# Two attention units share a PSUM bank for their values, and the mLSTM's small sums are done once for two units

## The chip, the cores and the metric

The kernel runs on one core of one Trainium2 chip. The metric is the device time of one execution in microseconds (us). Before the change it was 3861.58 us, the median of three runs (3859.82 to 3863.74).

## The reference, cut to what matters

The reference is a long chain of layers on 512 latent tokens and 256 context tokens of 1024 channels. Two places of it are touched. In the first layer, two attentions of 8 heads each run over the same 768 tokens; latent rows see all 768 keys, context rows the 256 context keys alone:

```python
def attend(q, k, v):
    ...
    s = jnp.einsum('bqgrd,bsgd->bgrqs', qi, k).astype(jnp.float32) * scale
    p = jax.nn.softmax(s, axis=-1).astype(v.dtype)
    return jnp.einsum('bgrqs,bsgd->bqgrd', p, v)
```

"GQA" has 8 query heads on 2 key/value heads of 64 channels; "MLA" has 8 heads with keys of 96 channels and values of 64. In the second layer an mLSTM runs in both directions over the sequence, and its result is divided by a sum of its own weights:

```python
den = w_inter * jnp.einsum('bhd,bhtd->bht', n, qc) + jnp.sum(s, axis=-1)
h = num / jnp.maximum(jnp.abs(den), jnp.exp(-m_t))[..., None]
```

## The kernel before, in words

One function builds each layer, and every engine executes its instructions in the order in which the Python code issues them. There is no scheduler: `pipeline` (L1660) walks over steps, and in each step calls a list of stages, each with a lag, so that stage `f` with lag 3 handles unit `u - 3` in step `u`. The order of that list is the order on every engine.

**Attention** (`run`, L1918, called for GQA at L2022 and for MLA at L2117). A unit is one head and one block of 128 query rows: 8 heads x 6 blocks = 48 units per attention. Blocks 0 to 3 are latent ("heavy", 768 keys), 4 and 5 context ("light", 256 keys). Per unit:

- `S`: scores into a two-bank PSUM tile `D` on TensorE, one step ahead (L1894 and L1895 for GQA; L1914 to L1916 for MLA).
- `X`: maximum and bias on VectorE (L1942, L1943), exponential on ScalarE (L1946).
- `R`: reciprocal of the sum on VectorE (L1950), scaling on GpSimd (L1951).
- `Tr`: transposes of the probabilities on TensorE (L1962) into banks `A` (4) and `B` (2).
- `CpB`, `CpA`: copies of these into the tile `pT`, by ScalarE (L1967) and VectorE (L1972).
- `PV`: the product with the values (L1981), six matmuls for a heavy unit and two for a light one, accumulating in bank `V`. Its stationary operand has 128 columns: two heads' values side by side (MLA), or the one head's values twice (GQA, copied twice by `twice`, L1794). So all 128 rows of the result are computed, and only the 64 of the unit's own head are used.
- `Ev`: the 64 rows are split into a rounded high part (L1988) and the rest (L1989), both on VectorE.
- `prep`, `preH`, `preL`: transposes of the next head's queries and keys, and their split.

There is one bank `V`: the next `PV` cannot begin before `Ev` has read the last one.

**mLSTM** (`ml_heads`, L2327). A unit is one head and one block of 128 rows, 8 x 4 = 32 units. `decay` makes exponentials on ScalarE two steps ahead (L2402 to L2405), `S_` the scores on TensorE (L2392, L2393), and `M` (L2407) multiplies them on VectorE in three instructions with running sums (L2414). Then follow four small instructions on one or two columns: L2415 adds two sums, L2418 takes the magnitude, L2419 the maximum with `em`, L2420 the reciprocal. With these, `R` scales and adds on GpSimd (L2425 to L2428), `Tr` transposes (L2436), `CpA` copies on ScalarE (L2440), `PV` multiplies with the values (L2447), `Ev` reads the result on ScalarE (L2454, L2455). GpSimd makes the masks of the next head too (L2364). After the last unit, `wout_k` gives TensorE matmuls of the output projection between the last stages.

Of the kernel before, what the change touches and what calls it, by code (L numbers as in the profile page):

```python
# [12 lines left out]
F32 = mybir.dt.float32  # L13
F32R = mybir.dt.float32r
AF = mybir.ActivationFunctionType
# [166 lines left out]
class Kernel:  # L182
# [1503 lines left out]
    def attn(self):  # L1686
# [103 lines left out]
        def to(dst, d0):  # L1790

            return lambda t, n: dst[:, t, d0:d0 + n]

        def twice(t, n):  # L1794

            return G2[:, t, 128:].rearrange("p (g u n) -> p u g n", g=2, u=2)
# [11 lines left out]
        for g, cut in enumerate(cuts):  # L1808
            n = sum(c[2] for c in cut)
            o = self.six()  # L1810
            self.nat(("ai", g), 4, x, range(6), [b[:, :n] for b in o], mid=mid[g > 0], extra=extra[g],
                     ada=(0, 1, 1, 1)[g])
            for t in range(6):
                for dst, c0, m in cut:
                    a, b = dst(t, m), o[t][:, c0:c0 + m]
                    if dst is twice:
                        b = b.rearrange("p (g n) -> p g n", g=2).unsqueeze(1).to_broadcast([P, 2, 2, 64])
# [31 lines left out]

        def prep_g(h, i, b):  # L1850

            if (i == 1 and 2 <= h < 4) or (i == 2 and h == 3):
# [12 lines left out]
            for c in range(2):  # L1865
                o = slice(t0 * P, t1 * P)
                r.append((b[c * 64:c * 64 + 64, :(t1 - t0) * P],
                          (qs[c * 64:c * 64 + 64, c, o], qs[64 - c * 64:128 - c * 64, c, o])))
            return r

        def lat_kv(h, i, b):

            g = [self.v("mla_kva_g", c) for c in range(2)]
            if i == 1:
                c = h - 2
# [42 lines left out]
        def run(prep, scores, value, sc, out, bg, tail):  # L1918


            self.psum(A=2, B=1, V=1)
            esW, pW = self.pool(self.nm("attW"), "left")
            units = [(h, t) for h in range(8) for t in range(6)]
            U = [dict(W=768 if t < 4 else 256) for h, t in units]

            def S(u):
                h, t = units[u]
                d = U[u]
                d["s"] = b = self.bank("D").rearrange("p a b -> p (a b)")
                if t == 4 and h < 7:  # L1930
                    U[u - 1]["pre"] = prep(h + 1, 2, b[:, 0:512])
# [31 lines left out]

            def CpB(u):
                d = U[u]
                d["p"] = p = pW.tile([P, TT], F32, tag="pT", bufs=3, name=self.nm("pT"))
                nc.scalar.activation(p[:, T:], d.pop("B")[:, :TC], AF.Copy)  # L1967

            def CpA(u):
# [2 lines left out]
                    nc.vector.tensor_copy(d["p"][:, :T], d.pop("A"))  # L1972

            def PV(u):
                h, t = units[u]
                d = U[u]
                d["o"] = q = self.bank("V")[:, 0:P]
                p = d.pop("p")
                j0 = 6 - d["W"] // P
                for j in range(j0, 6):  # L1980
                    nc.tensor.matmul(q, value(h, j), p[:, j * P:(j + 1) * P], start=j == j0, stop=j == 5)  # L1981

            def Ev(u):
                h, t = units[u]
                r = slice(h % 2 * 64, h % 2 * 64 + 64)
                q = U[u].pop("o")[r]
                hi, lo = (z[r, h // 2, t * P:(t + 1) * P] for z in out)
                nc.vector.tensor_copy(hi, q)  # L1988
                nc.vector.tensor_tensor(lo, q, hi, ALU.subtract)  # L1989

            def preT(u):
                h, t = units[u]
                if t < 2 and h < 7:
                    U[u]["pre"] = prep(h + 1, t, self.bank("A"))
# [9 lines left out]
                    else:  # L2004
                        nc.vector.tensor_tensor(dst[1], src, dst[0], ALU.subtract)

            for i in range(3):
                U[0]["pre"] = prep(0, i, self.bank("AAV"[i]))
# [318 lines left out]
    def ml_heads(self, x, esi, pi, es7, openx):  # L2327
# [67 lines left out]
        def decay(u):  # L2395
            h, j = units[u]
            d, E, dm = U[u], st[h]["U"], st[h]["dm"]
            e = til([P, 1152], "mE", 5)
# [8 lines left out]
        def M(u):  # L2407
            h, j = units[u]
            d = U[u]
            q, f, b = d.pop("s"), d["f"], d["b"]  # L2410
            den = til([P, 4], "mden", 3)
            n = d["Wb"] - TC
            for i, (o, c) in enumerate(((b[:, n:], slice(0, TC)), (b[:, :n], slice(d["c"], TT)), (f, slice(0, d["Wf"])))):
                nc.vector.scalar_tensor_tensor(o, q[:, c], 0.125, o, ALU.mult, ALU.mult, accum_out=den[:, 2 - i:3 - i])  # L2414
# [70 lines left out]
        def last(f):  # L2485
            return at(3, f)
# [4 lines left out]
        for c in range(8):  # L2491
# [4 lines left out]
            if c == 7:  # L2496
# [12 lines left out]
        decay(0)  # L2509
        decay(1)  # L2510
        S_(0)
        self.pipeline(len(units), ((3, CpA), (4, Ev), (-2, decay), (0, at(0, keysH, 1)), (0, at(1, queriesH, 1)),
                                   (10, last(n6h)), (5, last(n2)), (0, M), (0, at(1, keysL, 1)),
                                   (0, at(2, queriesL, 1)), (8, last(n3)), (12, last(n6l)), (1, R),
                                   (0, at(1, masks, 1)), (9, last(n4)), (-1, S_), (2, Tr), (3, PV), (9, last(n5)),
                                   (0, at(2, load, 2)), (3, at(3, load_v, 2)), (4, last(load_o))),
                      lambda i: self.wout_k("mw", hl, min(i, 6)) if i < 6 or i == 8 else None)
        es.close()
        esp.close()
        self.psum(M=2, A=2)  # L2520
# [233 lines left out]
```

## Time and profile before

| | |
|---|---|
| median of three runs | 3861.58 us |
| the profiled execution's own time | 3859.96 us |
| its span, first to last instruction | 3858.2 us |
| TensorE / VectorE / ScalarE / GpSimd busy, whole span | 95% / 68% / 41% / 19% |
| granted TensorE clock, whole span | 0.981 |
| GQA, first to last maximum (L1942) | 178.45 to 291.96 us |
| MLA, first to last maximum (L1942) | 354.98 to 476.63 us |
| mLSTM, first to last reciprocal (L2420) | 1367.66 to 1486.69 us |

The busy time of TensorE is a sum over stages of very different make, and a matmul's duration in the trace includes its latency, so that neighbours overlap. What a matmul costs is the distance between the starts of two neighbours. A matmul of two plain float32 operands stands twice in the trace, as two passes, each with its own weight load ("PEld"): 6 matmuls of one heavy `PV` are 12 records. Transposes are one pass.

### The profile page before, as it was taken

The numbers are of one execution on the slowest core, as the hardware profiler recorded it, in microseconds if no ns is written. First come the engines' busy times: TensorE is split into PE (matmuls) and PEld (weight loads), VectorE is DVE, ScalarE is ACT, GpSimd is POOL, SyncE is SP. The second block draws the span as 40 slices with busy tenths as digits, with TensorE's granted clock in tenths as the row PEclk, the third lists the DMA queues.
The fourth block names the chain that finished last, engine by engine and source line by source line (L and its number), as shares of the span: only waits on it lengthen the run. The fifth ranks groups of instructions, "written<-read, shape, count | busy, mean of one in ns | idle before, by whom it ended". The sixth has DMA issues, their size and how long they took to land. (4 is left out here: it accounts for less than half of the span.)

```text
span 3858.2 us, 54617 instructions
## 1 busy us (share of the span) xinstructions
PE 3656.6 (95%) x21148; PEld 3150.7 (82%) x21148; DVE 2621.0 (68%) x4287; ACT 1577.4 (41%) x2606; POOL 720.7 (19%) x755
## 2 busy tenths in 40 slices
PE   7898999999999978999999998999999999889999
PEld 5887978888887777877789886788977998678898
DVE  7887877765646286544477777677765777766776
ACT  2354523222225275422344447444443444464443
POOL 6334231000012074100100016100020000460000
PEclk8999999999999999999999999999999999899999
DMA  5300043433422442233333322333334333213332
GB/s 176 107 1 23 1 148 95 125 112 118 137 68 88 139 134 77 82 90 90 90 98 102 96 78 81 97 87 96 95 114 124 98 99 99 83 42 102 98 103 75
DMA packets 570400, 363.48 MB, mean 94 GB/s; under 512 B 17719, under 2 KB 546605, under 8 KB 570141
## 3 DMA queue, kind: packets, MB, share of 16 engines
q1 hardware_dynamic: 564317, 346.21, 30.7%
q0 software_dynamic: 3520, 9.59, 0.8%
q8 instruction: 167, 2.74, 0.3%
q10 hardware_dynamic: 2304, 4.20, 0.3%
q14 instruction: 92, 0.75, 0.1%
HBM read 345.72 MB, written 14.20 MB: 93 GB/s over the span
## 5 line engine op out<-in xcount | busy, mean ns | idle before, releaser
L135 DVE TENSOR_TENSOR wl<-ws,wh 128x1024 fp32r<-128x1024 f32 (+3 forms) x474 | 583.3, 1240 | 313.6 <-ACT wh L132 311.2
L132 ACT ACTIVATE wh<-ws 128x1024 fp32r<-128x1024 f32 (+3 forms) x474 | 457.6, 978 | 588.5 <-DVE ws L454 257.3
L562 PE MATMUL D<-ah,wl 128*128 128x256 f32 x1344 | 380.2, 283 | 11.1 <-DVE wl L135 11.1
L560 PE MATMUL D<-ah,wh 128*128 128x256 f32 x1344 | 377.1, 281 | 1.6 <-DVE gu L602 1.6
L561 PE MATMUL D<-al,wh 128*128 128x256 f32 x1344 | 376.4, 280 | 0.9 <-DVE al L495 0.9
L539 PE MATMUL M<-hz,wh 128*128 128x512 f32 x704 | 279.9, 398 | 2.2 <-DVE xT L545 2.2
L540 PE MATMUL M<-hz,wh 128*128 128x512 f32 x704 | 280.4, 398 | 1.0 <-DVE hz L638 0.9
L541 PE MATMUL M<-hz,wl 128*128 128x512 f32 x704 | 278.8, 396 | 0.0
L562 PEld LDWEIGHTS D<-ah,wl 128*128 128x128 f32 x1344 | 252.8, 188 | 18.5 <-DVE wl L135 18.5
L341 POOL TENSOR_TENSOR acc<-acc,t 128x512 f32<-128x512 f32 x36 | 46.9, 1303 | 1171.4 <-ACT t L340 1171.4
L560 PEld LDWEIGHTS D<-ah,wh 128*128 128x128 f32 x1344 | 252.9, 188 | 6.0 <-ACT wh L132 1.9
L561 PEld LDWEIGHTS D<-al,wh 128*128 128x128 f32 x1344 | 252.8, 188 | 5.0 <-DVE al L495 1.3
L321 PE MATMUL D<-ah,wl 128*128 128x512 f32 (+1 forms) x616 | 242.8, 394 | 7.0 <-DVE wl L135 7.0
L317 PE MATMUL D<-ah,wh 128*128 128x512 f32 (+1 forms) x616 | 244.7, 397 | 3.0 <-ACT wh L132 2.7
L319 PE MATMUL D<-al,wh 128*128 128x512 f32 (+1 forms) x616 | 242.8, 394 | 0.8 <-POOL al L2676 0.6
L303 POOL TENSOR_TENSOR hl<-t,hh 128x768 fp32r<-128x768 f32 (+1 forms) x44 | 70.0, 1590 | 797.9 <-ACT hh L302 737.1
L1349 DVE SCALAR_TENSOR_TENSOR as<-ws,S,as 128x256 f32<-128x256 f32 x448 | 202.7, 504 | 3.5
L560 PE MATMUL E<-ah,wh 128*128 128x256 f32 x672 | 188.9, 281 | 6.8 <-ACT t L590 4.0
L562 PE MATMUL E<-ah,wl 128*128 128x256 f32 x672 | 189.9, 283 | 4.7 <-DVE wl L135 4.7
L561 PE MATMUL E<-al,wh 128*128 128x256 f32 x672 | 188.1, 280 | 0.0
L317 PE MATMUL D<-x7h,wh 128*128 128x512 f32 (+1 forms) x464 | 183.8, 399 | 3.0 <-ACT x7h L2671 1.6
L321 PE MATMUL D<-x7h,wl 128*128 128x512 f32 (+1 forms) x464 | 181.4, 394 | 1.1 <-DVE wl L135 1.1
(711 smaller groups left out, 9696.6 us busy)
## 6 DMA issues: line engine op xcount, KB each, us to landing
ws<-in_ffn_w_up_dram SPq DMA_DIRECT2D x104, 512.0 KB
ws<-in_ada_w_dram SPq DMA_DIRECT2D x88, 512.0 KB
t<-in_ffn_w_down_dram SPq DMA_DIRECT2D x128, 256.0 KB
ws<-in_ffn_w_gate_dram SPq DMA_DIRECT2D x88, 256.0 KB
ws<-in_ffn_w_up_dram SPq DMA_DIRECT2D x88, 256.0 KB
wz<-in_ffn_w_gate_dram SPq DMA_DIRECT2D x56, 256.0 KB
wz<-in_ffn_w_up_dram SPq DMA_DIRECT2D x56, 256.0 KB
ws<-in_ffn_w_down_dram SPq DMA_DIRECT2D x32, 384.0 KB
```

What stands on the lines that cost most here:

```text
L132: self.nc.scalar.activation(h[:, :n], t[:, :n], AF.Copy)
L135: self.nc.vector.tensor_tensor(l[:, :n], t[:, :n], h[:, :n], ALU.subtract)
L317: nc.tensor.matmul(o, wh[:, kw + k], xh[:, k0 + k, s], start=a, stop=False)
L319: nc.tensor.matmul(o, wh[:, kw + k], xl[:, k0 + k, s], start=False, stop=False)
L321: nc.tensor.matmul(o, wl[:, kw + k], xh[:, k0 + k, s], start=False, stop=z)
L539: nc.tensor.matmul(q, wh[:, k], h[:, 0, i], start=a, stop=False)
L540: nc.tensor.matmul(q, wh[:, k], h[:, 1, i], start=False, stop=False)
L541: nc.tensor.matmul(q, wl[:, k], h[:, 0, i], start=False, stop=z)
L560: nc.tensor.matmul(o, wh[:, u, k], xh(k0 + k, s), start=start and k == 0, stop=False, skip_group_check=True)
L561: nc.tensor.matmul(o, wh[:, u, k], xl(k0 + k, s), start=False, stop=False, skip_group_check=True)
L562: nc.tensor.matmul(o, wl[:, u, k], xh(k0 + k, s), start=False, stop=stop and k == 3, skip_group_check=True)
L1349: nc.vector.scalar_tensor_tensor(t, w[:, kk], c, t, ALU.mult, ALU.add)
```

## The change

`PV` waits for two units and works on both at once. The stationary operand is now the unit's own 64 columns of values; the first unit's result goes to partitions 0 to 63 of bank `V`, the second's to 64 to 127, and the matmuls of the two alternate. In the built program these matmuls carry a tile of 128 x 64 at column 0 or 64 of the array, where all others around them carry 128 x 128. GQA's units are reordered so that a pair is two heads with the same block (`by_head`); an MLA pair is two blocks of one head. `Ev` becomes `EvH` on ScalarE (lag 5) and `EvL` on VectorE (lag 6), for GQA one instruction of 128 rows for the pair, for MLA two of 64. The tile `pT` has four buffers instead of three. In the mLSTM the four small instructions are issued in every second step, for two units, and everything from `R` on comes one step later; `mE` has six buffers instead of five.

```diff
-        G2 = pG.tile([P, 6, 384], F32, name="rawG2")
+        G2 = pG.tile([P, 6, 256], F32, name="rawG2")
...
-        cuts = (((to(G, 0), 0, 384),), ((to(G, 384), 0, 128), (to(G2, 0), 128, 128), (twice, 256, 128)),
+        cuts = (((to(G, 0), 0, 384),), ((to(G, 384), 0, 128), (to(G2, 0), 128, 128), (to(G2, 128), 256, 128)),
...
-            units = [(h, t) for h in range(8) for t in range(6)]
+            units = ([(h + c, t) for h in (0, 2, 4, 6) for t in range(6) for c in range(2)] if by_head else
+                     [(h, t) for h in range(8) for t in range(6)])
...
             def PV(u):
+                if u % 2 == 0:
+                    return
                 h, t = units[u]
-                d = U[u]
-                d["o"] = q = self.bank("V")[:, 0:P]
-                p = d.pop("p")
-                j0 = 6 - d["W"] // P
+                U[u]["o"] = q = self.bank("V")[:, 0:P]
+                ps = [U[u - 1 + c].pop("p") for c in range(2)]
+                j0 = 6 - U[u]["W"] // P
                 for j in range(j0, 6):
-                    nc.tensor.matmul(q, value(h, j), p[:, j * P:(j + 1) * P], start=j == j0, stop=j == 5)
-
-            def Ev(u):
+                    for c in range(2):
+                        nc.tensor.matmul(q[c * 64:c * 64 + 64], value(h, j), ps[c][:, j * P:(j + 1) * P],
+                                         start=j == j0, stop=j == 5)
+
+            def outs(u):
                 h, t = units[u]
-                r = slice(h % 2 * 64, h % 2 * 64 + 64)
-                q = U[u].pop("o")[r]
-                hi, lo = (z[r, h // 2, t * P:(t + 1) * P] for z in out)
-                nc.vector.tensor_copy(hi, q)
-                nc.vector.tensor_tensor(lo, q, hi, ALU.subtract)
+                if u % 2 == 0:
+                    return []
+                if by_head:
+                    return [(U[u]["o"], h // 2, slice(0, P), t)]
+                return [(U[u]["o"][c * 64:c * 64 + 64], h // 2, slice(h % 2 * 64, h % 2 * 64 + 64), t - 1 + c)
+                        for c in range(2)]
+
+            def EvH(u):
+                for q, k, r, t in outs(u):
+                    nc.scalar.activation(out[0][r, k, t * P:(t + 1) * P], q, AF.Copy)
+
+            def EvL(u):
+                for q, k, r, t in outs(u):
+                    ts_ = slice(t * P, (t + 1) * P)
+                    nc.vector.tensor_tensor(out[1][r, k, ts_], q, out[0][r, k, ts_], ALU.subtract)
...
-            self.pipeline(len(units), ((1, preH), (3, CpB), (0, X), (1, R), (5, Ev), (3, CpA), (1, preL), (0, bg),
-                                       (-1, S), (0, preT), (2, Tr), (4, PV)), tail)
+            self.pipeline(len(units), ((1, preH), (3, CpB), (0, X), (1, R), (6, EvL), (5, EvH), (3, CpA), (1, preL),
+                                       (0, bg), (-1, S), (0, preT), (2, Tr), (4, PV)), tail)
...
-        run(prep_g, scores_g, lambda h, j: G2[:, j, 128 + h // 4 * P:256 + h // 4 * P], scG, self.oG,
+        run(True, prep_g, scores_g, lambda h, j: G2[:, j, 128 + h // 4 * 64:192 + h // 4 * 64], scG, self.oG,
...
-        run(prep_m, scores_m, lambda h, j: V[:, j, h // 2 * 2:h // 2 * 2 + 2].rearrange("p h n -> p (h n)"), scM,
+        run(False, prep_m, scores_m, lambda h, j: V[:, j, h], scM,
...
-            den = til([P, 4], "mden", 3)
+            k = u % 2
+            if k == 0:
+                U[u + 1]["den"] = d["den"] = til([P, 2, 4], "mden", 2)
...
-            nc.vector.tensor_tensor(den[:, 1:2], den[:, 1:2], den[:, 2:3], ALU.add)
-            den = den[:, 0:2]
-            d["r"] = r = self.tmp(2, tag="mb", bufs=3)
-            nc.vector.scalar_tensor_tensor(r, den, -1.0, den, ALU.mult, ALU.max)
-            nc.vector.tensor_tensor(r, r, self.em[:, j, h:h + 33:32], ALU.max)
-            nc.vector.reciprocal(r, r)
+            if k:
+
+                r = til([P, 2, 2], "mr", 2)
+                nc.vector.tensor_tensor(den[:, :, 1:2], den[:, :, 1:2], den[:, :, 2:3], ALU.add)
+                nc.vector.scalar_tensor_tensor(r, den[:, :, 0:2], -1.0, den[:, :, 0:2], ALU.mult, ALU.max)
+                nc.vector.tensor_tensor(r, r, self.em[:, j - 1:j + 1, h:h + 33:32], ALU.max)
+                nc.vector.reciprocal(r, r)
+                U[u - 1]["r"], d["r"] = r[:, 0], r[:, 1]
```

Where the instructions stand now. TensorE in the first GQA head, from one heavy unit's scores to the next one's, before (`V` the value bank, `pT` the transposed probabilities, `rawG` the values):

```order
L1894 MATMUL D_1865<-gkh,qs_1705 128x512
L1895 MATMUL D_1865<-gkl,qs_1705 128x512
L1894 MATMUL D_1865<-gkh,qs_1705 128x256
L1895 MATMUL D_1865<-gkl,qs_1705 128x256
L1962 MATMUL A_1870<-ident,t_1791 128x128 x4
L1962 MATMUL B_1875<-ident,t_1791 128x128 x2
L1981 MATMUL V_1878<-pT_1812,rawG_100 128x128 x6
L1894 MATMUL D_1899<-gkh,qs_1705 128x512
```

The same engine now, from the transposes of one step on:

```order
L1958 MATMUL A_1878<-ident,t_1803 128x128 x4
L1958 MATMUL B_1883<-ident,t_1803 128x128 x2
L1980 MATMUL V_1886<-pT_1797,rawG_100 64x128
L1980 MATMUL V_1886<-pT_1826,rawG_100 64x128
L1980 MATMUL V_1886<-pT_1797,rawG_100 64x128
L1980 MATMUL V_1886<-pT_1826,rawG_100 64x128
...
L1888 MATMUL D_1912<-gkh,qs_1705 128x512
L1889 MATMUL D_1912<-gkl,qs_1705 128x512
L1888 MATMUL D_1912<-gkh,qs_1705 128x256
L1889 MATMUL D_1912<-gkl,qs_1705 128x256
L1958 MATMUL A_1918<-ident,t_1832 128x128 x4
```

Twelve matmuls with 64 result rows, alternating between the two units' probabilities, stand in every second step; in the other steps the transposes are followed directly by scores.

VectorE in the mLSTM, one unit and the start of the next, before (`mE` the decays, `mden` the sums, `D` the scores):

```order
L2414 SCALAR_TENSOR_TENSOR mE_12447,mden_12557<-D_12517,mE_12447 128x256
L2414 SCALAR_TENSOR_TENSOR mE_12447,mden_12557<-D_12517,mE_12447 128x512
L2414 SCALAR_TENSOR_TENSOR mE_12447,mden_12557<-D_12517,mE_12447 128x384
L2415 TENSOR_TENSOR mden_12557<-mden_12557 128x1
L2418 SCALAR_TENSOR_TENSOR t_12562<-mden_12557 128x2
L2419 TENSOR_TENSOR t_12562<-t_12562,mlem 128x2
L2420 RECIPROCAL t_12562<-t_12562 128x2
L2414 SCALAR_TENSOR_TENSOR mE_12499,mden_12601<-D_12570,mE_12499 128x256
```

And now, two units:

```order
L2433 SCALAR_TENSOR_TENSOR mE_12311,mden_12407<-D_12373,mE_12311 128x256
L2433 SCALAR_TENSOR_TENSOR mE_12311,mden_12407<-D_12373,mE_12311 128x512
L2433 SCALAR_TENSOR_TENSOR mE_12311,mden_12407<-D_12373,mE_12311 128x384
L958 TENSOR_SCALAR t_12451<-mss_12257 128x4
L2433 SCALAR_TENSOR_TENSOR mE_12356,mden_12407<-D_12415,mE_12356 128x256
L2433 SCALAR_TENSOR_TENSOR mE_12356,mden_12407<-D_12415,mE_12356 128x384
L2433 SCALAR_TENSOR_TENSOR mE_12356,mden_12407<-D_12415,mE_12356 128x512
L2437 TENSOR_TENSOR mden_12407<-mden_12407 128x2
L2438 SCALAR_TENSOR_TENSOR mr_12457<-mden_12407 128x4
L2439 TENSOR_TENSOR mr_12457<-mr_12457,mlem 128x4
L2440 RECIPROCAL mr_12457<-mr_12457 128x4
```

The four small instructions stand once behind six products instead of once behind three, on twice as many columns; the rest keeps its place.

## Rows read from the trace of the kernel before

**Rows 1.** Windows, two heads each: GQA, GQA, MLA, MLA, mLSTM; columns in the header.

```profile
core 0: us, PE busy (x) PEld busy (x) DVE busy (x) ACT busy (x) POOL busy (x), PEclk, DMA share, GB/s
202.69:230.57 27.88, 26.21 (x201) 23.70 (x199) 24.78 (x70) 15.50 (x37) 7.63 (x11) 1.00 0.01 1
230.57:257.00 26.43, 25.14 (x193) 23.11 (x194) 22.81 (x67) 16.07 (x39) 8.94 (x12) 1.00 0.01 2
381.54:413.95 32.41, 31.61 (x255) 30.17 (x254) 26.84 (x76) 18.32 (x42) 9.18 (x12) 1.00 0.01 2
413.95:446.35 32.40, 31.59 (x255) 30.16 (x254) 26.84 (x75) 18.32 (x42) 9.18 (x12) 1.00 0.01 2
1419.91:1452.35 32.44, 24.38 (x187) 22.05 (x185) 30.81 (x93) 27.81 (x76) 27.42 (x38) 1.00 0.47 133
```

**Rows 2.** Timeline of PE, one heavy MLA step; start, length, engine, line, operation, count.

```profile
389.78 1.50 PE L1981 MATMUL V<-pT,mv 128*128 128x128 f32 x12
...
391.82 0.28 PE L1914 MATMUL D<-mqh 96*128 96x256 f32 x1
391.94 0.28 PE L1915 MATMUL D<-mql,mqh 96*128 96x256 f32 x1
...
392.17 0.60 PE L1962 MATMUL A<-ident,t 128*128 128x128 f32 x4
392.61 0.38 PE L1962 MATMUL B<-ident,t 128*128 128x128 f32 x2
392.83 0.61 PE L1981 MATMUL V<-pT,mv 128*128 128x128 f32 x4
```

**Rows 3.** Timeline of PE's weight loads, one heavy GQA unit.

```profile
203.99 1.42 PEld L1981 LDWEIGHTS V<-pT,rawG 128*128 128x128 f32 x12 [0.67 <-PE B L1962]
```

**Rows 4.** Timeline of PE, a late attention with operands of 64 rows.

```profile
3403.92 0.62 PE L1125 MATMUL D<-KS,qs 64*128 64x256 f32 x6
3404.38 0.28 PE L1129 MATMUL D<-mrow 64*128 64x256 f32 x2
3404.59 0.55 PE L1159 MATMUL A<-ident,E 128*128 128x128 f32 x3
3405.52 0.49 PE L1171 MATMUL V<-dv,t 128*128 128x128 f32 x2 [0.37 <-ACT do L1179]
3405.93 0.80 PE L1125 MATMUL D<-KS,qs 64*128 64x384 f32 x6
```

**Rows 5.** Groups by line and shape, VectorE, MLA, two heads; busy us, mean ns, idle.

```profile
L1989 DVE TENSOR_TENSOR o<-V,o 64x128 fp32r<-64x128 f32 x12 | 3.5, 288 | 0.4
L1988 DVE CAST o<-V 64x128 fp32r<-64x128 f32 x12 | 3.4, 284 | 3.8 <-PE V L1981 3.7
```

**Rows 6.** Groups by line and shape, VectorE, mLSTM, two heads.

```profile
L2415 DVE TENSOR_TENSOR mden<-mden 128x1 f32<-128x1 f32 x8 | 3.8, 474 | 0.0
L2418 DVE SCALAR_TENSOR_TENSOR t<-mden 128x2 f32<-128x2 f32 x8 | 3.8, 472 | 0.8
L2419 DVE TENSOR_TENSOR t<-t,mlem 128x2 f32<-128x2 f32 x8 | 3.3, 409 | 0.3
L2420 DVE RECIPROCAL t<-t 128x2 f32<-128x2 f32 x9 | 1.5, 166 | 0.3
```

**Rows 7.** Groups by line, ScalarE, mLSTM, two heads.

```profile
L2454 ACT ACTIVATE mO<-V 128x128 f32<-128x128 f32 x9 | 2.5, 278 | 3.4 <-PE B L2470 3.4
```

**Rows 8.** Waits in the MLA stretch of two heads: who for whom, total us, times, longest.

```profile
DVE o L1988 <- PE V L1981: 3.7, 6, 0.7
PE V L1981 <- DVE o L1989: 0.8, 2, 0.5
```

**Rows 9.** Windows after the mLSTM's last unit.

```profile
1488.00:1492.00 4.00, 4.00 (x22) 3.96 (x21) 2.35 (x4) 2.36 (x7) 3.72 (x4) 0.57 0.01 2
1492.00:1496.00 4.00, 4.00 (x27) 3.45 (x26) 0.00 (x0) 1.54 (x5) 0.88 (x2) 1.00 0.45 135
```

More of the change, by code (lines that the diff above doesn't have):

```diff
@@ L1792, in to @@
             return lambda t, n: dst[:, t, d0:d0 + n]
-        def twice(t, n):
-            return G2[:, t, 128:].rearrange("p (g u n) -> p u g n", g=2, u=2)
-        cuts = (((to(G, 0), 0, 384),), ((to(G, 384), 0, 128), (to(G2, 0), 128, 128), (twice, 256, 128)),
+        cuts = (((to(G, 0), 0, 384),), ((to(G, 384), 0, 128), (to(G2, 0), 128, 128), (to(G2, 128), 256, 128)),
                 ((to(M, 0), 0, 384),), ((to(M2, 0), 0, 256), (to(kr6, 0), 256, 32)))
@@ L1815, in attn @@
                     a, b = dst(t, m), o[t][:, c0:c0 + m]
-                    if dst is twice:
-                        b = b.rearrange("p (g n) -> p g n", g=2).unsqueeze(1).to_broadcast([P, 2, 2, 64])
                     if t % 2 and g != 2:
@@ L1850, in prep_g @@
         def prep_g(h, i, b):
-            if (i == 1 and 2 <= h < 4) or (i == 2 and h == 3):
+            if (i == 1 and 4 <= h < 6) or (i == 2 and h == 5):
                 return lat_kv(h, i, b)
@@ L1874, in lat_kv @@
             if i == 1:
-                c = h - 2
+                c = h - 4
                 for t in range(4):
@@ L1916, in scores_m, with run @@
             nc.tensor.matmul(o, ql[0:96, ts_], kh_[0:96, c0:c1], start=False, stop=True)
-        def run(prep, scores, value, sc, out, bg, tail):
+        def run(by_head, prep, scores, value, sc, out, bg, tail):
             self.psum(A=2, B=1, V=1)
             esW, pW = self.pool(self.nm("attW"), "left")
-            units = [(h, t) for h in range(8) for t in range(6)]
+            units = ([(h + c, t) for h in (0, 2, 4, 6) for t in range(6) for c in range(2)] if by_head else
+                     [(h, t) for h in range(8) for t in range(6)])
             U = [dict(W=768 if t < 4 else 256) for h, t in units]
@@ L1929, in S @@
                 d["s"] = b = self.bank("D").rearrange("p a b -> p (a b)")
-                if t == 4 and h < 7:
-                    U[u - 1]["pre"] = prep(h + 1, 2, b[:, 0:512])
+                if t == 4 and h + by_head < 7:
+                    U[u - 1]["pre"] = prep(h + 1 + by_head, 2, b[:, 0:512])
                 if d["W"] == 768:
@@ L1965, in CpB @@
                 d = U[u]
-                d["p"] = p = pW.tile([P, TT], F32, tag="pT", bufs=3, name=self.nm("pT"))
+                d["p"] = p = pW.tile([P, TT], F32, tag="pT", bufs=4, name=self.nm("pT"))
                 nc.scalar.activation(p[:, T:], d.pop("B")[:, :TC], AF.Copy)
@@ L1974, in PV @@
             def PV(u):
+                if u % 2 == 0:
+                    return
                 h, t = units[u]
-                d = U[u]
-                d["o"] = q = self.bank("V")[:, 0:P]
-                p = d.pop("p")
-                j0 = 6 - d["W"] // P
+                U[u]["o"] = q = self.bank("V")[:, 0:P]
+                ps = [U[u - 1 + c].pop("p") for c in range(2)]
+                j0 = 6 - U[u]["W"] // P
                 for j in range(j0, 6):
-                    nc.tensor.matmul(q, value(h, j), p[:, j * P:(j + 1) * P], start=j == j0, stop=j == 5)
-            def Ev(u):
+                    for c in range(2):
+                        nc.tensor.matmul(q[c * 64:c * 64 + 64], value(h, j), ps[c][:, j * P:(j + 1) * P],
+                                         start=j == j0, stop=j == 5)
+            def outs(u):
                 h, t = units[u]
-                r = slice(h % 2 * 64, h % 2 * 64 + 64)
-                q = U[u].pop("o")[r]
-                hi, lo = (z[r, h // 2, t * P:(t + 1) * P] for z in out)
-                nc.vector.tensor_copy(hi, q)
-                nc.vector.tensor_tensor(lo, q, hi, ALU.subtract)
-            def preT(u):
+                if u % 2 == 0:
[11 more added lines that the diff above has]
+                    nc.vector.tensor_tensor(out[1][r, k, ts_], q, out[0][r, k, ts_], ALU.subtract)
+            def preT(u):
+                if by_head:
+                    h, k = u // 12 * 2 + 2, u % 12
+                    if k in (0, 2, 4, 6) and h < 8:
+                        U[u]["pre"] = prep(h + k // 4, k // 2 % 2, self.bank("A"))
+                    return
                 h, t = units[u]
@@ L2005, in preL @@
                         nc.vector.tensor_tensor(dst[1], src, dst[0], ALU.subtract)
-            for i in range(3):
-                U[0]["pre"] = prep(0, i, self.bank("AAV"[i]))
+            for i in range(6 if by_head else 3):
+                U[0]["pre"] = prep(i // 3, i % 3, self.bank("AAVBAA"[i]))
                 preH(0)
@@ L2397, in decay @@
             d, E, dm = U[u], st[h]["U"], st[h]["dm"]
-            e = til([P, 1152], "mE", 5)
+            e = til([P, 1152], "mE", 6)
             c, Wf = d["c"], d["Wf"]
@@ L2410, in M @@
             q, f, b = d.pop("s"), d["f"], d["b"]
-            den = til([P, 4], "mden", 3)
+            k = u % 2
+            if k == 0:
+                U[u + 1]["den"] = d["den"] = til([P, 2, 4], "mden", 2)
+            den = d.pop("den")
             n = d["Wb"] - TC
             for i, (o, c) in enumerate(((b[:, n:], slice(0, TC)), (b[:, :n], slice(d["c"], TT)), (f, slice(0, d["Wf"])))):
-                nc.vector.scalar_tensor_tensor(o, q[:, c], 0.125, o, ALU.mult, ALU.mult, accum_out=den[:, 2 - i:3 - i])
-            nc.vector.tensor_tensor(den[:, 1:2], den[:, 1:2], den[:, 2:3], ALU.add)
-            den = den[:, 0:2]
-            d["r"] = r = self.tmp(2, tag="mb", bufs=3)
-            nc.vector.scalar_tensor_tensor(r, den, -1.0, den, ALU.mult, ALU.max)
-            nc.vector.tensor_tensor(r, r, self.em[:, j, h:h + 33:32], ALU.max)
-            nc.vector.reciprocal(r, r)
+                nc.vector.scalar_tensor_tensor(o, q[:, c], 0.125, o, ALU.mult, ALU.mult, accum_out=den[:, k, 2 - i:3 - i])
+            if k:
[5 more added lines that the diff above has]
+                U[u - 1]["r"], d["r"] = r[:, 0], r[:, 1]
         def R(u):
@@ L2511, in ml_heads @@
         S_(0)
[L2512 to L2517, printed above, removed]
+        self.pipeline(len(units), ((4, CpA), (5, Ev), (-2, decay), (0, at(0, keysH, 1)), (0, at(1, queriesH, 1)),
+                                   (11, last(n6h)), (6, last(n2)), (0, M), (0, at(1, keysL, 1)),
+                                   (0, at(2, queriesL, 1)), (9, last(n3)), (13, last(n6l)), (2, R),
+                                   (0, at(1, masks, 1)), (10, last(n4)), (-1, S_), (3, Tr), (4, PV), (10, last(n5)),
+                                   (0, at(2, load, 2)), (4, at(3, load_v, 2)), (5, last(load_o))),
+                      lambda i: self.wout_k("mw", hl, min(i, 6)) if i < 6 or i == 9 else None)
         es.close()
```

## Prediction

> **What bounds the kernel now.** I read the page first: TensorE is busy 95% of the span and no wait stands out, so the question is what each touched stage waits for. I then took, from the starts of the maxima and reciprocals, stretches of two whole heads in the steady part of each stage and asked for the busy time of every engine in them [rows 1]. In the MLA stretches TensorE is busy 31.61 of 32.41 us and VectorE 26.84: TensorE is the bound. In GQA it is 26.21 of 27.88 and 25.14 of 26.43, with VectorE at 24.78 and 22.81: TensorE again, VectorE close behind. In the mLSTM VectorE is busy 30.81 of 32.44, ahead of ScalarE (27.81), GpSimd (27.42) and TensorE (24.38). The granted clock is 1.00 in all five, the upper of its two levels (2.4 GHz). The waits agree: in MLA VectorE waits for the value product (3.7 us in six times), and TensorE for the release of bank V only 0.8 us [rows 8]. So whatever shortens TensorE counts in the two attentions, and whatever shortens VectorE counts in the mLSTM. Each attention has four such stretches (8 heads), and so has the mLSTM.
>
> **The change part by part.**
>
> *The value product.* The twelve weight loads of one heavy unit take 1.42 us from the first start to the last end, the last one 0.19: (1.42 - 0.19) / 11 = 0.112 us per pass [rows 3]; four passes of a light unit give the same, their successor standing some 0.45 us later [rows 2]. Two heads have 8 heavy and 4 light units: 8 x 6 + 4 x 2 = 56 matmuls, 112 passes, 12.54 us of TensorE per stretch. The change leaves the number of matmuls and the columns that stream through (128) as they are; what it alters is that each uses half of the array's columns, so that two may run at once.
>
> Whether they do, the attentions do not show: all matmuls there use all columns. The nearest rows are those of a late attention whose operands have 64 rows and which alternates the two halves of the rows [rows 4]. There two matmuls of 256 columns take 0.28 us together, which is what one alone takes [rows 2]; six of them take 0.62 us. One after another, at the 0.12 us between neighbours of 256 columns [rows 2], six would take 5 x 0.12 + 0.28 = 0.88. So halves of rows run side by side. For halves of columns I take the same, 0.056 us per pass, since this is the nearest row; the bounds are 0.112 (one after another), and above that if the load of the weights comes out of cover.
>
> Going into and out of such a tile costs something. The six of 256 columns should take 2 x 0.12 + 0.28 = 0.52 and take 0.62: 0.10 lost. Before the six of 384 the last of two preceding passes starts 0.49 - 0.28 = 0.21 after 3405.52, so with 0.11 for it the next could start at 3405.84 and starts at 3405.93: 0.09. Behind the pair at 3404.38 the next matmul starts 0.21 later instead of 0.12: 0.09 [rows 4]. Together 0.28 us per group. There are six groups per stretch: 1.7 us. The product then costs 56 x 0.112 + 1.7 = 8.0 us instead of 12.54: TensorE loses 4.5 us per stretch.
>
> The Trainium skill speaks against this ("TensorE: Matmul & The Clock Gate", Part 3, "What overlaps and what doesn't"): a weight load overlaps a running matmul only where their row groups differ, and the two halves here share all rows. By that, every slot of two passes would pay a load in the open. If that load is the 0.10 us of the first slot above, a slot costs 0.21 and the product gains nothing. The trace does not show it for halves of columns; the loads of full-width matmuls, which share rows as well, do lie under their predecessors [rows 3]. The same page reports 2.38 times for three column tiles. I make it part of the second rival.
>
> *Ev.* The high part (284 ns, 12 per stretch) leaves VectorE, and the rest (288 ns) is halved for GQA, where one instruction of 128 rows serves two units [rows 5]; rows lie side by side in the engine, so I leave its length. VectorE loses 3.4 + 1.7 = 5.1 us per GQA stretch and 3.4 per MLA stretch. ScalarE gets 6 copies of 128 rows for GQA and 12 of 64 for MLA; the nearest is a 128x128 copy out of PSUM at 278 ns [rows 7]: 1.7 and 3.3 us. It has room, 15.50 and 18.32 of a stretch [rows 1]. In its queue the exponential of the next unit stands behind such a copy, which waits for the product of the step before; I count up to 0.1 us per pair for that. The next product waits for the subtraction as it waited for `Ev`, now once per two units.
>
> New loads per stretch: GQA TensorE 25.7 - 4.5 = 21.2 (mean of the two), VectorE 23.8 - 5.1 = 18.7, ScalarE 17.5. MLA TensorE 31.6 - 4.5 = 27.1, VectorE 23.4, ScalarE 21.6. TensorE stays the bound in both. Its idle time was 1.5 us in GQA and 0.8 in MLA; with the product in every second step only the load is less even, and two tiles D allow one step of lead, so I take 1.8 and 1.0: stretches of 23.0 (from 27.15) and 28.1 (from 32.4). Over four stretches: 4 x 4.15 = 16.6 and 4 x 4.3 = 17.2 us.
>
> *The small sums.* The four instructions take 474 + 472 + 409 + 166 ns and the idle time before them adds (0.8 + 0.3 + 0.3) / 8 = 0.17 us: 1.69 us per unit [rows 6]. Columns hardly matter (474 for one, 472 for two), so half of them go: 4 x 1.69 = 6.8 us per stretch, and VectorE falls to 24.0. ScalarE (27.8) and GpSimd (27.4) are next. With the idle time of today, 1.6, the stretch is 29.4 instead of 32.4. Four stretches, less half of one for the start: 3.5 x 3.0 = 10.5. GpSimd then has two units to scale behind the last sums instead of one, some 2.6 us; TensorE has projection matmuls to do there and is busy without a gap [rows 9], so I charge 1.5: 9 us.
>
> *Without effect:* the narrower copies of the GQA values (six, beside the next matmuls), the buffers, the order of the preparations (the same instructions in other steps).
>
> Sum: 16.6 + 17.2 + 9 = 42.8. Against the profiled execution's 3859.96 us that is 3817.2; this execution is 1.6 below the median of the runs, so I predict 3819. The likeliest case's own range: each attention from 9 (if most of the gap between product and chain is lost) to 25 (switching free, 6.3 x 4), the mLSTM 2 to 16 (down to ScalarE's 27.8): 3797 to 3838 with the ends not all at once.
>
> **The rivals.**
>
> *The halves run in turn, or side by side with each load in the open.* Then the product costs 12.5 us and the switching 1.7 on top. GQA: TensorE 27.4, with 0.7 idle 28.1, +1.0 per stretch; MLA 33.3 + 0.5, +1.4 per stretch; 8 stretches +10, mLSTM -9: 3861 to 3863. For it: no row has halves of columns, and the operands are plain float32 in two passes, the first of which blocks its own half. Against it: halves of rows do run side by side.
>
> *Slower: in turn, and each load in the open.* Place: the product in TensorE. Price: 0.10 us on each of 112 passes, 11.2, and 1.7: 12.9 us per stretch, all of it on the bound of both attentions, with VectorE's relief worth nothing: 8 x 12.9 = 103, less 9: 3955. It decides from the point where a pass costs over (12.54 - 1.7 + 1.1) / 112 = 0.107 us, the 1.1 being the mLSTM's 9 us spread over the 8 stretches. For it: the first slot in rows 4 shows what an open load costs. Against it: only the first slot does.
>
> *The product gets short, but a chain takes over* (maximum, exponential, scaling, transposes, copy, each on another engine, with one step of lead): each attention gains 1.5 us per stretch, the mLSTM 3 in all since ScalarE and GpSimd were nearly as busy: 15 us, 3846. For it: TensorE's and VectorE's loads come within 4 us. Against it: both were nearly full before and kept to within 5% of TensorE's load.
>
> **How the numbers follow.** Forecast 0.64, second case (no gain in the product) 0.16, slower 0.08, chain 0.12. A measurement of this kernel can tell some 0.2% from no change, 7.7 us: faster below 3853.9, slower above 3869.3. Faster: 0.64 + 0.10 of the chain + 0.04 of the second case = 0.78; same: 0.09 of the second case and 0.02 of the chain = 0.11; slower: 0.08 and 0.03 = 0.11. The range leaves out the slower case, three quarters of the second and the lower tip: 3797 to 3858.
>
> **What would show it.** Right: the passes of the two halves start in pairs, within some ns of each other, pair after pair about 0.11 us apart; GQA's stretch of two heads is near 23 us and MLA's near 28; VectorE's small sums stand 16 times, not 32, and the mLSTM's stretch is near 29.4 with ScalarE and GpSimd fuller than VectorE. Wrong: 24 starts evenly spread over 2.7 us or more in a heavy pair, or TensorE idle by several us per stretch.

## The result and the profile after

The changed kernel takes 3818.84 us (median of four runs, 3816.71 to 3822.65), the kernel before 3862.09 beside it: ratio 0.989, interval 0.9872 to 0.9907. 3819 was forecast. The profiled execution took 3818.78 us, span 3817.0 against 3858.2.

**Where the 41 us lie.** I matched instructions that both kernels have, line by line, and took how much earlier each starts. The two kernels stand within 0.1 us of each other when GQA begins; at its end the changed one is 19.4 us ahead, at MLA's first transposes 18.8 and behind MLA 28.1, at the first matmul of the mLSTM 30.4 and behind its last normalization 43.8, at the end 41.2. So GQA gave 19.4 us, MLA 9.3, the mLSTM 13.3; the forecast had 16.6, 17.2 and 9. The sum is right, the parts are not; MLA's part, moreover, differs from execution to execution (last section).

The windows of two heads after (GQA, GQA, MLA, mLSTM; columns as in [rows 1]; the second MLA window, 29.56 us, is like the first):

```profile
203.91:230.91 27.00, 24.29 (x228) 20.24 (x227) 22.11 (x59) 20.19 (x52) 9.52 (x13) 1.00 0.01 1
230.91:255.90 24.99, 22.25 (x215) 18.85 (x214) 20.15 (x55) 17.85 (x47) 8.84 (x13) 1.00 0.01 2
364.05:393.61 29.56, 27.34 (x252) 23.76 (x252) 23.78 (x63) 21.15 (x55) 9.16 (x12) 1.00 0.01 2
1397.24:1425.87 28.63, 23.70 (x184) 21.83 (x184) 25.53 (x77) 26.72 (x71) 27.96 (x39) 1.00 0.40 111
```

Here a mistake of mine shows: the two GQA windows of [rows 1] hold eleven units each, not twelve. Cut from one maximum (L1942) to the twelfth behind it, before had 30.87 and 29.22 us:

```profile
207.37:238.24 30.87, 28.98 (x224) 26.45 (x223) 27.00 (x76) 18.18 (x44) 9.19 (x12) 1.00 0.01 1
238.24:267.46 29.22, 27.91 (x216) 25.55 (x215) 25.49 (x73) 16.91 (x41) 9.19 (x12) 1.00 0.01 2
```

A window on a loop is to be checked by the count of an instruction that occurs once per turn. TensorE was the bound by either cut, and the stretch lost 3.9 and 4.2 us where 4.15 were forecast. But the 23 us that the prediction gives as GQA's sign came from the short windows: 27.0 and 25.0 were measured, and in them TensorE sits idle for 2.7 us, not 1.8. In MLA it went from 32.4 to 29.56, not 28.1: TensorE's busy time came out as forecast (27.34 against 27.1), but it now sits idle for 2.2 us, not 1.0. In the mLSTM VectorE is no longer the fullest; GpSimd is, 27.96 of 28.63.

The value product of a heavy pair in MLA, timeline of PE (start, length, engine, line, operation, count):

```profile
380.56 0.38 PE L1958 MATMUL B<-ident,t 128*128 128x128 f32 x2
380.87 1.53 PE L1980 MATMUL V<-pT,mv 128*64 128x128 f32 x24
382.33 0.50 PE L1908 MATMUL D<-mqh 96*128 96x512 f32 x1
```

24 passes take 1.46 us to the next matmul's start. Before, 12 passes that start at 389.78 [rows 2] took 1.26, for the next matmul then is

```profile
391.04 0.48 PE L1914 MATMUL D<-mqh 96*128 96x512 f32 x1
```

Single records show pairs 5 to 8 ns apart (191.402 and 191.408, 191.562 and 191.568, 191.671 and 191.678 us) and, behind a first slot of 0.160 us, one pair every 0.109 us. The waits of the MLA stretch and of the mLSTM stretch (who for whom, total us, times, longest):

```profile
DVE t L1938 <- PE D L1910: 4.1, 4, 1.2
...
PE D L1908 <- DVE mql L2021: 2.2, 2, 1.1
```

```profile
PE T L2457 <- POOL mE L2449: 4.9, 6, 1.4
```

In each head of MLA TensorE now waits 1.1 us for the low part of the next head's context keys; what VectorE waited for was the value product [rows 8], and now it is the scores behind one. In the mLSTM the transposes wait for GpSimd's last add. The small sums there stand 16 times, as wanted, but the second got longer (579 ns, was 472 [rows 6]):

```profile
L2438 DVE SCALAR_TENSOR_TENSOR mr<-mden 128x4 f32<-128x4 f32 x4 | 2.3, 579 | 0.4
L2439 DVE TENSOR_TENSOR mr<-mr,mlem 128x4 f32<-128x4 f32 x4 | 1.6, 410 | 0.1
...
L2437 DVE TENSOR_TENSOR mden<-mden 128x2 f32<-128x2 f32 x4 | 0.7, 173 | 0.0
```

### The profile page after: what moved, and what is told of

It reads as the page before. It is cut to its first block, busy times and chain, and to the rows that moved or that the text cites. A ratio compares the mean times of both kernels' runs of the same rounds, so it can differ in the third digit from the quotient of the medians.

```text
span 3817.0 us, 54418 instructions
## 1 busy us (share of the span) xinstructions
PE 3619.6 (95%) x21148; PEld 3100.9 (81%) x21148; DVE 2564.8 (67%) x4103; ACT 1594.1 (42%) x2678; POOL 722.6 (19%) x755
## 5 line engine op out<-in xcount | busy, mean ns | idle before, releaser
L319 PE MATMUL D<-x7l,wh 128*128 128x512 f32 (+1 forms) x464 | 181.6, 394 | 0.6 <-DVE x7l L2699 0.6
```

What stands on the lines that cost most here:

```text
L319: nc.tensor.matmul(o, wh[:, kw + k], xl[:, k0 + k, s], start=False, stop=False)
```

## The experiments

All were timed beside the kernel before. Steps of 1 to 2 us that lie outside the changed stages differ from execution to execution (shown at the end), so below the stages are compared in the profiles, by the lead over before that a kernel gains in each; the changed kernel's are 19.4, 9.3 and 13.3 us.

### The two halves of the change

First kernel: `ml_heads` as before. Second: everything ahead of it as before.

> The change in both attentions alone; the mLSTM as before. Theory (the two parts are independent): the two traces give 29.9 us up to the mLSTM's start, so about 3862.1 - 30 = 3832 us, and the mLSTM's first to last maximum-and-sum as long as before. Rival (the mLSTM's gain is partly owed to what comes before it, a fuller clock or earlier loads): a time nearer to 3819 than to 3832 would need it; or the attention's gain is partly given back later: 3840 or more.

> The change in the mLSTM alone; both attentions as before. Theory (independent parts): 13.3 us of the two traces, so about 3849 us. Rival (half of the small sums is worth the 9 us that I predicted, the rest of the 13 is noise of the milestones): 3853.

Measured: 3831.38 us (ratio 0.9918, 0.9904 to 0.9931) and 3852.55 (0.9967, 0.9954 to 0.998). By its time the second lies nearer to the rival's 3853 than to 3849, but its five runs reach from 3846 to 3858; its trace decides: 13.2 us gained in the mLSTM and 0.6 in the attentions. The first gains 19.6 us in GQA, 11.8 in MLA and 0.4 in the mLSTM. The parts are independent and add up within the scatter. That MLA gains 11.8 here and 9.3 in the changed kernel, with the same attention code, is taken up in the last section.

### Do the halves run side by side

```diff
-                for j in range(j0, 6):
-                    for c in range(2):
+                for c in range(2):
+                    for j in range(j0, 6):
```

> The changed kernel, but the value product issues all matmuls of the first unit and then all of the second, instead of alternating. Same instructions, same waits on other engines. Theory (TensorE starts matmuls in order, so only alternating halves run side by side, and that is the attentions' gain): one heavy pair takes 23 slots of 0.109 us instead of 12, a light one 7 instead of 4, which is 4 x 1.2 + 2 x 0.33 = 5.5 us of TensorE per stretch of two heads, of which the 1 to 2 us that TensorE now idles may take a part: 8 x 3.5 to 8 x 5.5, 28 to 44 us slower than the changed kernel: 3847 to 3863. Rival (the gain is VectorE's relief by moving the high part to ScalarE, the side-by-side run is worth little): under 8 us slower, 3819 to 3827.

Measured: 3849.8 us (0.9965, 0.9953 to 0.9978), 31 us above the changed kernel, with the same instructions, as the theory had it. GQA still gains 7.3 us, MLA loses 5.5. The heavy pair's timeline, then the MLA stretch:

```profile
386.92 2.45 PE L1980 MATMUL V<-pT,mv 128*64 128x128 f32 x24
389.30 0.50 PE L1908 MATMUL D<-mqh 96*128 96x512 f32 x1
```

```profile
378.89:412.17 33.28, 31.07 (x252) 27.49 (x252) 23.80 (x64) 21.36 (x55) 9.19 (x12) 1.00 0.00 1
```

2.38 us to the next start instead of 1.46. From GQA's first unit to MLA's end this kernel is 1.2 us ahead of the one before: with the halves in turn the rest of the change is worth next to nothing to the attentions together. The prediction's second case, the halves in turn, was priced too high: a loss of 10 us in the attentions, where 1.2 were gained. The 7.3 us that GQA keeps come from the rest of the change there; which part of it gives them was not separated.

### Grouped-query attention without the new order of units

```diff
-        run(True, prep_g, ...
+        run(False, prep_g, ...
```

and `lat_kv` under the heads of before.

> The changed kernel, but grouped-query attention pairs two blocks of one head (as the latent attention does) instead of the same block of two heads, in the order of units of before. Theory: two evictions of 64 rows replace one of 128, about 12 more VectorE and 12 more ScalarE instructions of some 0.14 us per two heads, both beside TensorE's 23 us of 25, so the steady stretches change by less than 1 us each; the drain at the end loses what it won (4.8 us) because its last units are no longer four light ones: 3823 to 3828. Rival: the reorder gives nothing, and the pairs alone give it all: 3818 to 3820. Other rival: the interleaved heads cost time in the steady part (two preparations fall together), so that the time falls below 3817.

Measured: 3833.93 us (0.9924, 0.9911 to 0.9936). All three expectations missed: GQA gains 7.3 us, not 19.4, and most of the loss lies between the first and the last maximum (108.8 us here, 98.9 in the changed kernel). Its two windows and two of its waits:

```profile
208.05:237.98 29.93, 25.29 (x227) 20.94 (x225) 23.88 (x64) 21.30 (x55) 9.15 (x12) 0.96 0.00 1
237.98:266.40 28.42, 24.61 (x212) 20.21 (x211) 22.27 (x61) 20.03 (x52) 9.17 (x12) 0.92 0.01 2
```

```profile
PE D L1888 <- ACT pT L1963: 1.7, 1, 1.7
PE D L1888 <- DVE qs L2021: 1.5, 1, 1.5
```

TensorE waits 1.5 and 1.7 us at a time. Behind each of three waits of 1.54 us (they end at 206.35, 236.28 and 264.70) the granted clock falls, behind the one of 1.69 us it does not; the mean is 0.96 and 0.92 where the changed kernel has 1.00. So pairing two heads, with four light units in a row, is worth 12 of GQA's 19 us, in steady steps above all; what I had taken for the order's whole gain, the light units at the end, is the smaller part. The kernel takes back three things at once (the order of the units, the steps in which the preparations fall, the one eviction for two units), and which of them counts is not shown; the evictions alone are 12 of 283 ns on VectorE per stretch, not some 0.14 us each, where the changed kernel has 6 of 274. Nor do these 12 us add to the 12 that GQA lost with the halves in turn: either way the same 7.3 are left.

### What the mLSTM's 13 us are

The first puts the sums back to each unit and keeps the later steps; the second adds work to GpSimd:

```diff
+            nc.gpsimd.tensor_tensor(til([P, P], "mdum", 1), b[:, :P], b[:, :P], ALU.add)
             nc.gpsimd.tensor_tensor(f[:, c:], f[:, c:], b[:, :P], ALU.add)
```

> The changed kernel with one thing put back: the mLSTM's four small sums (add, absolute value, floor, reciprocal) are computed for each unit again, 32 per two heads instead of 16; the step of slack between a unit's decays and its use stays. Theory A: the mLSTM's 13 us come from the VectorE time that the paired sums save (about 16 instructions of 0.17 to 0.58 us per two heads), so nearly all of them go back: the stretch of two heads returns from 28.6 to about 32 us and the time is 3832 (3829 to 3835). Rival B: the gain is the added slack, the sums are off the path since GpSimd sets the pace (28.0 us busy of 28.6): 3819 to 3822.

> The changed kernel with one more GpSimd instruction per unit of the mLSTM: an add of 128x128 values into a scratch tile that nothing reads (0.457 us by the row of the same shape, 32 of them). Theory: after the change GpSimd sets the mLSTM's pace (27.96 us busy of 28.63 per two heads), so all 14.6 us of it show: 3831 to 3835. Rival: the four engines' chain sets it, with slack on GpSimd: 3819 to 3823.

Measured: 3833.84 us (0.9921, 0.9908 to 0.9935) and 3832.23 (0.9919, 0.9906 to 0.9933). Their stretches of two heads, sums first:

```profile
1400.87:1432.61 31.74, 23.85 (x184) 21.99 (x184) 30.23 (x93) 26.92 (x70) 27.55 (x39) 1.00 0.44 116
```

```profile
1398.88:1430.35 31.47, 24.02 (x174) 21.91 (x173) 25.90 (x78) 25.58 (x68) 30.80 (x46) 0.95 0.48 126
```

With the sums per unit VectorE is the bound again and the mLSTM gains 4.7 us: of the 13.3, the sums give 8.6 and the later steps 4.7. Where these 4.7 lie shows in the lead along the stage: 1.1 us up to the last unit's transposes, 3.6 behind them. The same 3.6 us stand behind the last unit in every kernel with the later steps, and none in the one with the mLSTM as before. Two things that cost time there before are gone. TensorE sat idle for 1.98 us ahead of the transposes of the output, and its clock then was 0.57 in the first window of [rows 9]; now twelve projection matmuls stand ahead of these transposes, which do not wait, and the clock is 1.00 (before, then the changed kernel and its window):

```profile
1487.50 0.66 PE L2470 MATMUL B<-ident,mO 128*128 128x128 f32 x4 [1.98 <-DVE mO L2464]
```

```profile
1448.02 0.60 PE L2491 MATMUL B<-ident,mO 128*128 128x128 f32 x4
```

```profile
1440.00:1465.00 25.00, 23.60 (x146) 20.46 (x145) 7.51 (x10) 9.29 (x23) 11.21 (x14) 1.00 0.22 68
```

How much each of the two is worth was not separated.

With one more instruction per unit on GpSimd (433 ns each in the trace, some 14 us in all) the mLSTM gains 0.3 us: 13.0 of them show. The stretch and GpSimd's busy time both grow by 2.84 us. After the change GpSimd sets the pace.

### MLA's wait for the context keys

Four kernels try to take it away. One issues all low parts (`preL`) ahead of VectorE's copy (`CpA`); one issues only the context's, ahead of the light unit's maximum; one moves the context's transposes a step forward, into bank A; one gives the copy in front of it to ScalarE.

```diff
-(5, EvH), (3, CpA), (1, preL),
+(5, EvH), (1, preL), (3, CpA),
...
-((1, preH), (3, CpB), (0, X),
+((1, preH), (1, preE), (3, CpB), (0, X),
...
-                if t == 4 and h + by_head < 7:
+                if by_head and t == 4 and h < 6:
...
-                if t < 2 and h < 7:
+                if t < 3 and h < 7:
...
-((1, preH), (3, CpB), (0, X),
+((1, preH), (3, CpB), (3, CpA1), (0, X),
```

> The changed kernel with the low half of the prepared operands (preL) issued ahead of the copy CpA on VectorE, in both attentions. In the changed kernel's MLA TensorE waits 1.1 us per head for that split of the context keys, and VectorE then 1.1 and 0.9 us for scores. Theory (this wait at the head's boundary is where MLA's missing gain went): the split comes 0.68 us earlier, MLA gains about 0.7 us per head, 5 us in all, 3814. Rival (MLA is bound by the uneven load of TensorE, with the value product in every second step, and the wait only moves): within 1.5 us of 3819.

> The changed kernel, but in the latent attention the low part of the context's queries and keys (one VectorE instruction per head) is issued ahead of the light unit's maximum and exponential, not behind it, and so right after its high part; the splits that lie in the other bank stay where they were. Theory: TensorE's wait of 1.1 us per head before the next head's first scores goes, and VectorE's wait for the scores behind the value product shrinks with it, so that a latent attention's two-head stretch goes from 29.56 to about 27.5 us: 3810 (3807 to 3814). Rival: the light unit's maximum is now 0.7 us later and the wait only moves to its transposes: 3818 to 3822.

> The changed kernel, but in the latent attention the next head's context queries and keys are transposed into the bank of the heavy units' transposes (A), with the third block, and no longer into the scores' bank with the first light one: its split then stands one step earlier, ahead of the light units, on ScalarE and VectorE both. Theory (the split of the context keys is late, and TensorE waits 1.1 us per head for it): that wait goes and the stretch of two heads falls from 29.56 to 27.5 us or less, 3810 to 3813 in all. Rival: VectorE as such paces the step of the light units, so that the 1.1 us turns up as another wait: 3818 to 3822. Other rival: the bank A is taken by the transposes of the block before, TensorE waits for its eviction, and the time is 3823 or more.

> The changed kernel, but in the latent attention the copy of the second block's transposes (128x512, one per head) is made by ScalarE ahead of its exponential, and no longer by VectorE ahead of the split of the context keys. Theory: in the light steps VectorE's queue paces (maximum, low part, copy, split one behind the other, 0.67 us for the copy), while ScalarE has 8 us idle of 29.6; the split and TensorE's scores behind it come about 0.7 us sooner in each head, the stretch of two heads falls from 29.56 to about 28.2 us, the latent attention by 4 to 5 us, to 3814 (3811 to 3818). Rival: the exponential of the light unit waits for the copy, and its chain takes the place: stretch 29.3 or more, 3817 to 3822.

Measured: 3821.4 us (0.9888, 0.9873 to 0.9903), 3825.78 (0.9899, 0.9884 to 0.9914), 3820.5 (0.9892, 0.9879 to 0.9906) and 3824.31 (0.9889, 0.9872 to 0.9905): none can be told from the changed kernel. The stretch of two heads was 29.59, 29.31, 29.63 and 29.60 us. My theory, that VectorE's queue ahead of the split is the cause, fell four times. In the first the split waits for the light unit's exponential; in the second TensorE does; in the third TensorE waits for bank A, which the context's transposes now share; in the fourth the split waits again as in the first (a wait each, and a row of VectorE's timeline):

```profile
DVE mql L2021 <- ACT t L1942: 1.4, 2, 0.7
```

```profile
PEld D L1908 <- ACT t L1943: 2.4, 2, 1.2
```

```profile
PE A L1958 <- DVE pT L1968: 2.5, 2, 1.3
```

```profile
394.01 0.69 DVE L2026 TENSOR_TENSOR mql<-D,mqh 96x512 fp32r<-96x512 f32 x1 [0.71 <-ACT t L1942]
```

What they may share: the next head's first scores go into the tile D that the light unit has. That is free only when the unit's maximum, its exponential and, but for the third kernel, the split are through, in the changed kernel 2.1 us behind the maximum's start. In the changed kernel the copy and the exponential end within 0.1 us of each other (392.89 and 392.88) and the split begins behind both, at 393.00, so that taking one away leaves the other. Before, TensorE waited in such a stretch for bank V alone (0.8 us, [rows 8]); that the longer product of each unit hid this chain is inferred. A third score tile would test it (D now has four banks, A two, B and V one each; a third D would need two more) and was not tried. That this chain alone sets the stretch stays argued, not shown.

### The changed kernel again, and with a GpSimd add moved

```diff
-            nc.gpsimd.tensor_tensor(f[:, c:], f[:, c:], b[:, :P], ALU.add)
+            (nc.vector if u % 2 else nc.gpsimd).tensor_tensor(f[:, c:], f[:, c:], b[:, :P], ALU.add)
```

on top of the bank A kernel above.

> The changed kernel itself, beside the two kernels made from it: 3819 (3817 to 3823). If steps that lie outside the changed stages explain the scatter of the runs so far (in their profiles single steps of 1.5 us lie at different places of the program), its profile shows the same time for the two attentions and the mLSTM to 1 us as its first one (-19.4, -9.3 and -13.3 against before), and differs elsewhere.

> The same, and in the mLSTM every second unit's 128x128 add goes from GpSimd to VectorE (16 of 32). Theory: GpSimd, which sets the mLSTM's pace, loses 1.8 us of 28.0 per two heads, VectorE gains about 1.2 on 25.5, ScalarE has 26.7: the stretch falls by 1.2 to 1.8 us, 5 to 7 us less in all than the kernel without it (3803 to 3808 if the other edit holds). Rival: the engines are balanced, what GpSimd loses VectorE's chain takes: within 2 us of the kernel without it.

Measured: 3821.66 us (0.99, 0.9886 to 0.9914) and 3817.38 (0.9887, 0.9873 to 0.9901). The repeat has 19.8, 9.4 and 13.2 us in the stages, as expected. The moved add is no gain that can be told in the times. By the traces the mLSTM gains 15.0 us with it and 13.0 without, where 5 to 7 more were expected: the end of the stage gets shorter, but the stretch longer,

```profile
1395.21:1424.52 29.31, 24.22 (x184) 21.92 (x184) 28.77 (x80) 26.72 (x71) 27.57 (x35) 1.00 0.35 100
```

and VectorE, at 28.77, is the fullest again. The rival (within 2 us) held, at its edge; nothing tried beats the changed kernel beyond the scatter.

## Why the prediction was right, and where it was not

- **TensorE is the bound, and the halves run side by side: right, shown.** Pairs start 5 to 8 ns apart, a slot takes 0.109 us (0.112 forecast), and in turn the same product takes 2.38 us instead of 1.46. Four heavy pairs of 1.46 us and two light ones of 0.59 are 7.0 us per stretch, 8.0 forecast: switching costs (7.0 - 56 x 0.109) / 6 = 0.15 us a group, not 0.28. The rows of a late attention, halves of rows, were a good guide to halves of columns.
- **The rule of the Trainium skill** ("TensorE: Matmul & The Clock Gate", Part 3, "What overlaps and what doesn't"), by which a weight load overlaps a running matmul only where their row groups differ, is not borne out here: the halves share all rows, and two loads of 137 ns each fit into a slot of 109 ns.
- **GQA, 16.6 forecast, 19.4 measured.** The steady stretch came out as forecast (-3.9 and -4.2 against -4.15), partly by luck: the product got shorter than forecast, and TensorE's idle time rose by 0.8 and 1.4 us, not 0.3. First to last maximum shrinks by 14.6 us (113.51 to 98.88); missed were the 4.8 in what follows it, where the new order ends the stage with four light units. The step that failed is that the prediction gives the new order nothing ("the order of the preparations" without effect): without the pairs of heads and their order 12 us are gone.
- **MLA, 17.2 forecast, 9.3 measured: the mis-sized term is TensorE's idle time,** 2.2 us per stretch and not 1.0, the 1.1 us per head in front of the next head's first scores. I had allowed 0.2 for the less even load. Four stretches at 1.46 us are 5.8 of the missing 7.9. The rest comes and goes with the execution: where the granted clock does not fall in the first stretch (windows below), the same code gains 11.8 us. This is the third rival, a chain that takes over, in part; which chain stays argued.
- **The mLSTM, 9 forecast, 13.3 measured: the mis-sized term is the end of the stage.** Up to the last unit's transposes 9.7 us are gained, where 10.5 were forecast: VectorE's relief was over-sized (5.3 us per stretch, not 6.8), but the stretch fell to 28.63, not 29.4. Behind them I charged a loss of 1.5 us, and 3.6 were gained. TensorE does wait for GpSimd's last units there (1.40 us), as I had thought; but I read [rows 9] as "busy without a gap", and passed over the clock of 0.57 in that very row and the idle 1.98 us just ahead of it, which the later steps remove. That ScalarE and GpSimd would be fuller than VectorE was right.
- **The errors cancel:** +2.8, -7.9, +4.3. That the total agrees to 0.2 us is luck; the terms were off by up to 7.9, and MLA's alone moves by 2.5 between executions.

## What to carry to other kernels

Where a product uses half of the array's columns, two of them in halves of one bank cost little more than one (1.46 us against 1.26 here): alternate them pass by pass, not one after the other. Once an engine's load is cut in some steps of a loop only, ask what the shortest step's chain is: the gain may stop there, and here four moves of one wait each left another. Read the clock in a window as well as the busy time, at the end of a stage too. Which units stand beside each other can be worth as much as the faster operation.

## What the hardware showed that I had not expected

The value product's weight loads take 137 ns with 64 columns, where they took 192 with 128 (medians). The number of columns alone does not set this: the loads of the transposes, 128 columns too, take 141.

TensorE's clock fell behind some single waits and not behind others like them. In MLA's first stretch of the changed kernel TensorE waits 1.33 us at 346.5, and the windows behind it show the clock at 0.64 on average, between its two levels, and back at 1.00:

```profile
346.00:349.00 3.00, 1.67 (x10) 1.25 (x9) 2.78 (x9) 1.53 (x5) 1.33 (x2) 0.91 0.00 0
349.00:353.00 4.00, 4.00 (x34) 3.50 (x34) 1.78 (x4) 1.52 (x5) 0.53 (x2) 0.64 0.01 4
353.00:357.00 4.00, 4.00 (x36) 3.56 (x37) 2.80 (x7) 2.82 (x8) 0.91 (x1) 1.00 0.00 0
```

In the kernel with the change in the attentions alone, whose attention code is the same, the same wait stands and the clock stays at 1.00:

```profile
348.77 0.50 PE L1908 MATMUL D<-mqh 96*128 96x512 f32 x1 [1.33 <-DVE mql L2021]
```

```profile
350.00:354.00 4.00, 4.00 (x44) 3.53 (x43) 2.28 (x5) 1.90 (x5) 0.48 (x1) 1.00 0.02 4
```

MLA gains 11.8 us there, and 11.8 with the sums per unit, again with the same attention code and no fall; in the six traces of a side-by-side product in which it falls there MLA gains 9.2 to 9.4. With the context's transposes a step earlier that wait is 0.5 us, the clock stays at 1.00 and MLA gains 11.9; since the same happens without that edit, it is not shown to be its doing.

This accounts for part of the scatter too. In code that no kernel touches TensorE waits some 2 us for a weight's low part, 2.12 us in the changed kernel's repeat and 1.96 in the kernel with the copy on ScalarE. The first runs on at 1.00, the second does not and loses some 1.5 us (the same 4 us of each):

```profile
1769.00:1773.00 4.00, 3.90 (x17) 3.17 (x18) 3.21 (x5) 0.63 (x1) 0.00 (x0) 1.00 0.53 144
```

```profile
1769.00:1773.00 4.00, 4.00 (x12) 3.17 (x11) 2.58 (x4) 1.23 (x3) 0.00 (x0) 0.57 0.62 166
```

Why one execution meets it and the other not, no run here tells.
